# A hybrid encoder block on one core: the order of the first row blocks, the scale of V's second half, the queue of four stores, and the waits at the start of the MLP

## The chip, the cores and the metric

The kernel runs on one core of a Trainium2 chip. The metric is the device time of one execution in microseconds (us), given as the median of several runs. The engines are TensorE (PE in the profile; PEld are its weight loads), VectorE (DVE), ScalarE (ACT), GpSimd (POOL) and SyncE (SP, which here does nothing but issue DMAs). Each engine works through its own instruction queue strictly in program order; semaphores make it wait for the others. A wait at the head of a queue therefore holds everything behind it on that engine.

## The reference

One pre-norm encoder layer over 1024 tokens of width 1024, in float32. Cut to what matters:

```
u = rms_norm(x, norm1_g)
q, k, v, cb, cc, ch, ga, gb = split(u @ w_in)     # 512 columns each, ga and gb 1024
q, k = rms_norm(q) , rms_norm(k)                  # per head, 8 heads x 64
y_a = neighbourhood_attention(q, k, v, rpb) @ w_attn_branch
y_b = (cb * conv3(cc * ch)) @ w_conv_branch
x = x + (sigmoid(ga) * y_a + sigmoid(gb) * y_b) @ w_o
h = rms_norm(x, norm2_g) @ w_mlp_in               # 1024 x 1024 by 1024 x 4096
y = x + square(relu(h)) @ w_mlp_out               # 1024 x 4096 by 4096 x 1024
```

## The kernel before

**Numbers.** Every float32 operand of a matmul is split into two float16 parts, hi and lo, after a scaling by a power of two; a product is three passes (hi hi, hi lo, lo hi). ScalarE makes the hi part (a copy with scale, L291), VectorE the lo part (value times scale minus hi, L278). Tokens come in eight row blocks of 128; x is held in `xt`, its normed rows in `u16` (tile `u`), the turned rows, which the matmuls take, in `uT`.

**Weights.** A `Chunk` is a piece of a weight matrix, 2 to 4 raw tiles of up to 128x1024 float32. `Chunk.prep` (L230 to L293) makes the power of two for it and then its two parts. For V and the MLP the scale comes from the largest magnitude (VectorE scans each raw tile, L302); for the kinds Q, K, C and G it comes from the sum of squares (ScalarE squares each raw tile with an accumulated sum, L241; a tiny matmul with ones, `all_sum` L177 to L183, adds over the partitions; `gm2`, the square of the largest gain, bounds the result). V is two chunks (`half` 0 and 1). Of each of them GpSimd makes the lo part of the second raw tile, in two steps (scale, then subtract); VectorE makes that of the first. `Chunk.first`, `done` and `load_upto` let SyncE's queue issue the next weight loads as raw tiles come free: five raw buffers.

**The order.** It is written out by hand. Two lists of Python generators hold work for the vector engines: `bg` (weight chunks, advanced by `tick`) and `fg` (everything else, advanced by `step`). `unit` issues the matmuls of one group, then the late evictions of the unit before, and then so many steps and ticks. `apart(mark, n)` and `wait(n)` make a generator wait until n more units or steps have gone. So the numbers in the schedule decide where in each engine's queue an instruction stands.

**The beginning** (L515 to L562). `ln_step(b, n)` advances the norm of row block b: a square on ScalarE (L418), a chain of small VectorE operations (L391, L394, L396, L102, L400) with one ScalarE root (L392), the hi part of u on ScalarE (L421), the lo part on VectorE (L423). Blocks 0 to 2 are turned on TensorE (`ln_trans`, L429 to L435), blocks 3 to 7 by transposing DMAs (`ln_turn`). V's units (`v_unit`) are six of 256 columns, then five of 512; their results leave the PSUM banks by ScalarE (L509) and VectorE (L510). `sforms` (L468) makes, for four pairs of row blocks, the sums of rows that the gates' seven-product scheme needs: ScalarE scales the two xt blocks (L475), GpSimd adds (L481), ScalarE casts to hi (L483), VectorE makes lo (L485), and `sform_store` (L488) sends 1 MB to DRAM (`GS`). Then Q and K: eight units each of 24 matmuls, whose results ScalarE evicts (L578, L579, L596).

**The MLP's first half** (L1478 on). Weights and rows are combined so that one `quad` needs seven products instead of eight: `quad(q)` is seven groups of 12 matmuls, in the order 1, 6, 5, 4, 2, 7, 3, with its partial sums in the seven forms z[0] to z[6] of a tile `AS[q]` (two buffers, so quad q takes that of quad q-2). Quads 0 and 1 are done in two halves of 256 columns. After a quad's last group `h_done` (L1430) stands in `fg`: Relu and Square on ScalarE (L1432, L1434), then `sums` (L1159: four additions into forms 4 to 6, on VectorE for quads 0 and 1, on GpSimd later), then the store of all seven forms, 1792 KB, to `HS` from SyncE's queue (L1438). The buffer is free when the store has landed. Meanwhile the next weight chunks are prepared on ScalarE (L952, L961, L981), GpSimd (L966) and VectorE (L932, L933, L977), with `all_sum` (L179, L182) between.

Of the kernel before, what the change touches and what calls it, by code (L numbers as in the profile page):

```python
# [10 lines left out]
F32 = mybir.dt.float32  # L11
# [41 lines left out]
def encoder_block(ctx: ExitStack, tc: tile.TileContext, x, weights, cols, gqk, rel, masks, out):  # L53
# [166 lines left out]
    class Chunk:  # L220


        def __init__(self, kind, widths, tag, rows, half, more):
            self.kind, self.bank = kind, {"V": "o", "Q": "o", "K": "s", "C": "d"}.get(kind)
            self.tag, self.rows, self.widths, self.more = tag, rows, widths, more
            self.offs = []
            self.raw, self.ready, self.half, self.pool = [], more > 0, half, () if half is None else (1,)
            self.split = False

        def prep(self):  # L230
            n = len(self.widths)
            nk = sum(k for k, _ in self.widths)
            rm, a, b, s = (cols_of("prep", i) for i in (nk, 1, 1, 1))
            self.inv = keep()
            tot = sum(k * w for k, w in self.widths)
            if self.kind in "QKCG":
                self.parts = wsp.tile([128, 2, tot], F16, name="w16_ws", tag="ws")
                for p, (k, w) in enumerate(self.widths):
                    while len(self.raw) <= p:
                        yield WAIT  # L240
                    A.activation(self.parts[:, 1, :k * w].bitcast(BF16), self.raw[p][:, :k * w], AF.Square,  # L241
                                 accum_out=sc[:, at(rm, p)])
                    yield
                V.tensor_reduce(sc[:, a], sc[:, at(rm, 0, n)], axis=AX, op=OP.add)
                c = ones_col()
                V.tensor_tensor(c, sc[:, a], sc[:, gm2], op=OP.mult)
                yield from apart(units[0], 2 if self.kind == "Q" else 3)
                yield from all_sum(c, b, bank(self.bank) if self.bank else anybank(), 1e-36)
                yield from pow2_half(b, 14, s, self.inv, more=self.more)
            else:  # L250
                yield from self.largest(rm, a, b)
                yield from pow2(b, 14, s, self.inv, False, more=self.more)
            V.tensor_scalar(sc[:, rm], sc[:, self.rows], sc[:, s], None, op0=OP.mult)
# [15 lines left out]
            prev, scaled = None, {}  # L269
            for it in todo + [None]:  # L270
                if prev:
                    p, parts, f = prev
                    for o, m, c in parts:
                        hi, lo = (self.parts[:, w, f + o:f + o + m] for w in range(2))
                        if p in self.pool:
                            G.tensor_tensor(lo, scaled[p][:, o:o + m], hi, op=OP.subtract)
                        else:
                            V.scalar_tensor_tensor(lo, self.raw[p][:, o:o + m], sc[:, c:c + 1], hi,  # L278
                                                   op0=OP.mult, op1=OP.subtract)
                    done[0] += 1  # L280
                    load_upto(done[0] + 5)
                splitting[0] = True
                if it:
                    p, parts, f = it
                    if p in self.pool:
                        scaled[p] = w1p.tile([128, 1024], F32, name="scaled", bufs=1)
                        for o, m, c in parts:
                            G.tensor_scalar(scaled[p][:, o:o + m], self.raw[p][:, o:o + m], sc[:, c:c + 1], 1.0,
                                            op0=OP.mult, op1=OP.mult)
                    for o, m, c in parts:  # L290
                        A.activation(self.parts[:, 0, f + o:f + o + m], self.raw[p][:, o:o + m], AF.Copy,  # L291
                                     scale=sc[:, c:c + 1])
                prev = it  # L293
                self.split = it is None
                yield
# [191 lines left out]

    def sform_store(n, v):  # L488
        yield from apart(units[0], 1)
        SP.dma_start(GS[:, n], v)  # L490
        formed[0] = n + 1

    def ln_step(b, n=1):
# [19 lines left out]
                               for k in range(8) for sa, sw in PASSES]), post, steps, ticks)  # L513

    push(cV[0])  # L515
    ln_step(0, 2)
    tick()
    ln_step(0, 5)
    ln_step(1)
    tick(3)  # L520
    ln_step(0)
    ln_step(1)
    tick(4)
    ln_trans(u16[:, 0], 0, UT)
    flush()
    ln_step(1, 5)
    ln_step(1)
    ln_step(2, 2)
    push(cV[1])
    tick(1)  # L530
    v_unit(0, 0, 0, 0)
    ln_step(2, 4)
    ln_trans(u16[:, 1], 1, UT)
    ln_step(2, 1)
    tick(3)
    ln_step(2)
    tick(4)
    ln_step(3, 2)
    ln_trans(u16[:, 2], 2, UT)
    ln_step(3, 4)  # L540
    fg.append(qk_gain())
    fg.append(sforms())
    V.tensor_reduce(sc[:, gm2], sc[:, g1], axis=AX, op=OP.max, apply_absolute_value=True)
    mul(gm2, gm2, gm2)
    for p in range(11):
        if p == 3:
            flush()
            push(cQ)
        if 0 < p < 6:
            v_unit(p % 3, p // 3, 1, 2)  # L550
        elif p:
            v_unit(p - 3, None, 2, 4)
        for q in (p,) if p < 6 else (2 * p - 6, 2 * p - 5):
            c = q // 2 + 3
            if c < 8 and q % 2 == 0:
# [2 lines left out]
                turned[0] = c + 1  # L558
            if c < 7:
                ln_step(c + 1, 3)  # L560
    settle()
    flush()  # L562

# [624 lines left out]

    PART = ((0, 4), (4, 7))

    spare = []

    def pieces(n, part):

# [88 lines left out]
    def forms_m():  # L1283
# [9 lines left out]
        load_upto(done[0] + 5)  # L1293
        t2 = w4p.tile([128, 2, 512], F16, name="t2", bufs=1)
        t4 = w4p.tile([128, 2, 512], F16, name="t4", bufs=1)
        k4 = lambda v: v.rearrange("p (k c) -> p k c", k=4)
        flat = {0: lambda i: P1[0][:, 7, i], 1: lambda i: two[:, 0, i], 2: lambda i: two[:, 1, i],
                5: lambda i: t2[:, i], 6: lambda i: t4[:, i]}
# [130 lines left out]

    def h_done(q):  # L1430
        f = AS.pop(q)
        A.activation(f[:, 0:4], f[:, 0:4], AF.Relu)  # L1432
        yield
        A.activation(f[:, 0:4], f[:, 0:4], AF.Square, scale=sc[:, c1[q].inv],  # L1434
                     accum_out=sc[:, at(bsum[q // 4], q % 4)])
        yield
        yield from sums(f, G if q > 1 else V)
        SP.dma_start(HS[q // 4][:, :, q % 4], f)  # L1438
        live.remove(q)
# [7 lines left out]
    def quad(q, c0=0, c1=512):  # L1447
# [5 lines left out]
            AS[q] = w4p.tile([128, 7, 512], F32, name="as", tag="as")  # L1453
        ps = {}
        z = [AS[q][:, i, c0:c1] for i in range(7)]

        def post6(ps):
            V.tensor_tensor(z[5], ps[6], z[4], op=OP.add)  # L1458
# [280 lines left out]
```

## Time and profile before

| What | us |
|---|---|
| median of 3 runs | 1242.75 (1242.17 to 1243.26) |
| the profiled execution | 1241.45 |
| its span on the core | 1239.7 |
| TensorE busy | 1200.9 |
| VectorE busy | 930.0 |
| ScalarE busy | 765.2 |
| GpSimd busy | 425.5 |

The mean granted clock of TensorE over the span is 0.996 of full speed. The span is the time from the first to the last instruction in the trace; the execution's time is 1.75 us longer. In the rows of a timeline, the first number is the start, the second the duration of the group, then engine, line, operation, output<-inputs and shape; `x4` is the count; the bracket gives the idle time of that engine just before, and what ended it. In the rows of the windows come, for each engine, its busy time and its count of instructions, then the granted clock (1.00 is full), the share of the DMA engines and GB/s.

### The profile page before, as it was taken

The page shows a single profiled execution, that of the slowest core. Times are in us where ns is not written, and L with a number is a line of the kernel's source. Part 1 is how long each engine was busy: PE and PEld are TensorE (multiplying, and loading weights), DVE is VectorE, ACT ScalarE, POOL GpSimd, SP SyncE. Part 2 cuts the span into 40 slices and gives each one's busy share as a digit, 9 for nine tenths or more (in the row PEclk, how much of TensorE's full clock was granted, in tenths as well). Part 3 has the DMA queues.
Part 4 walks back from the last instruction along what each step waited for, and adds up shares of the span by engine and source line. Part 5 has one row for each costly group of instructions (what it writes and reads, how often), then busy time and mean ns, then how long its engine had stood idle before and what let it go on. Part 6 is the DMA issues. An engine that isn't in the chain of part 4 may idle for free.

```text
span 1239.7 us, 17066 instructions
## 1 busy us (share of the span) xinstructions
PE 1200.9 (97%) x6294; PEld 575.6 (46%) x6294; DVE 930.0 (75%) x1743; ACT 765.2 (62%) x1179; POOL 425.5 (34%) x289
## 2 busy tenths in 40 slices
PE   5989999999999999999999899999999999999998
PEld 3534444444444444444458344444444444444444
DVE  6668677988557777877877654564546999999997
ACT  6777577787474554536767877877765763645430
POOL 2440003111331111101003356556657473473562
PEclk8999999999999999999999999999999999999999
DMA  6557446656651211216096543553474744436202
GB/s 257 107 203 170 79 120 137 133 119 120 132 144 44 68 45 58 68 34 255 18 178 146 204 150 130 187 171 136 161 288 161 300 167 148 167 116 232 102 34 102
DMA packets 170868, 173.36 MB, mean 140 GB/s; under 512 B 131488, under 2 KB 132000, under 8 KB 166688
## 3 DMA queue, kind: packets, MB, share of 16 engines
q1 hardware_dynamic: 170784, 172.27, 47.0%
q8 instruction: 49, 0.80, 0.3%
q14 instruction: 35, 0.29, 0.1%
HBM read 102.51 MB, written 37.75 MB: 113 GB/s over the span
## 4 chain that ended last, share of the span: by engine, by line
PE 67%; DVE 18%; ACT 7%; issue 4%; DMA 1%; POOL 1%; SPq 0%; DVEq 0%; ACTq 0%; POOLq 0%
PE ps_d L188 26%; PE ps_s L188 20%; PE ps_o L188 18%; PE ps_d L859 3%; DVE sz L797 2%; DVE P L823 2%; DVE w_s L977 2%; DVE w_ws L278 1%; DVE ops L1572 1%; POOL sform L481 1%; DMA raw<-in_weights 1%; ACT w_ws L241 1%; ACT as L1432 1%; DVE sc L302 1%; DVE sg L1093 1%
## 5 line engine op out<-in xcount | busy, mean ns | idle before, releaser
L188 PEld LDWEIGHTS <-ops 128*128 128x128 f16 x1356 | 132.4, 98 | 159.5 <-issue 2.7
L188 PEld LDWEIGHTS <-w 128*128 128x128 f16 x1368 | 133.2, 98 | 145.7 <-issue 7.2
L859 PE MATMUL ps_d<-uT,w_ws 128*128 128x512 f16 x528 | 125.4, 379 | 0.0
L188 PE MATMUL ps_d<-ops 128*128 128x512 f16 (+1 forms) x528 | 118.4, 374 | 0.0
L188 PE MATMUL ps_s<-ops 128*128 128x512 f16 x492 | 113.2, 379 | 1.5 <-DVE ops L1572 1.1
L1563 ACT ACTIVATE ops<-hf,sc 128x2048 f16<-128x2048 f32 x26 | 52.0, 1998 | 93.7 <-PE ps_o L188 34.8
L966 POOL TENSOR_TENSOR tsum<-raw 128x512 f32<-128x512 f32 x28 | 45.5, 1637 | 156.5 <-ACT raw L952 145.8
L188 PEld LDWEIGHTS <-uT 128*128 128x128 f16 x648 | 65.0, 101 | 70.4 <-issue 5.6
L1159 POOL TENSOR_TENSOR as<-as 128x512 f32<-128x512 f32 x56 | 76.6, 1369 | 37.1 <-ACT as L1434 33.8
L188 PEld LDWEIGHTS <-w_s 128*128 128x128 f16 x588 | 56.8, 98 | 69.4 <-DVE w_s L977 1.9
L188 PE MATMUL ps_d<-u2x,w 128*128 128x512 f16 (+1 forms) x360 | 80.0, 372 | 0.0
L1565 DVE SCALAR_TENSOR_TENSOR ops<-hf,sc,ops 128x2048 f16<-128x2048 f32 x26 | 74.2, 2852 | 5.2 <-ACT ops L1563 5.2
L188 PE MATMUL ps_o<-ops 128*128 128x512 f16 x336 | 77.1, 379 | 0.0
L859 PEld LDWEIGHTS <-w_ws 128*128 128x128 f16 x528 | 50.8, 98 | 52.5
L188 PE MATMUL ps_o<-u2T,w 128*128 128x512 f16 (+1 forms) x324 | 71.7, 371 | 0.0
L952 ACT ACTIVATE raw<-raw,sc 128x256 f32<-128x256 f32 x172 | 70.8, 493 | 0.7 <-DMA raw<-in_weights 0.7
L966 POOL TENSOR_TENSOR gsum<-raw 128x512 f32<-128x512 f32 x14 | 18.9, 1371 | 131.7 <-issue 57.1
L981 ACT ACTIVATE w<-raw,sc 128x512 f16<-128x512 f32 (+1 forms) x28 | 24.6, 927 | 61.2 <-DVE sc L411 61.2
L188 PE MATMUL ps_s<-u2T,w 128*128 128x512 f16 (+1 forms) x252 | 54.2, 366 | 2.4 <-DVE as L1467 2.4
L1458 DVE TENSOR_TENSOR as<-ps_d,as 128x512 f32<-128x512 f32 (+1 forms) x15 | 10.1, 673 | 58.8 <-ACT as L1475 58.8
L806 ACT ACTIVATE sz<-sz,sc 128x384 f32<-128x384 f32 (+1 forms) x64 | 37.3, 582 | 26.9 <-DVE sc L797 13.5
L278 DVE SCALAR_TENSOR_TENSOR w_ws<-raw,sc,w_ws 128x512 f16<-128x512 f32 (+2 forms) x72 | 46.1, 690 | 2.4 <-ACT w_ws L291 2.4
(336 smaller groups left out, 2615.2 us busy)
## 6 DMA issues: line engine op xcount, KB each, us to landing
raw<-in_weights SPq DMA_DIRECT2D x89, 512.0 KB, 5.5
hs<-as SPq DMA_DIRECT2D x16, 1792.0 KB, 8.7
hf<-hs SPq DMA_DIRECT2D x26, 1024.0 KB, 6.5
w2x<-in_weights SPq DMA_DIRECT2D x16, 512.0 KB, 8.1
raw<-in_weights SPq DMA_DIRECT2D x16, 384.0 KB, 3.8
xt<-in_x SPq DMA_DIRECT2D x8, 512.0 KB, 9.9
gs<-s SPq DMA_DIRECT2D x4, 1024.0 KB, 6.2
x<-in_x SPq DMA_DIRECT2D x8, 512.0 KB, 10.0
```

The costliest lines, as they stand in the source:

```text
L188: T.matmul(ps, l, r, start=a, stop=b)
L278: V.scalar_tensor_tensor(lo, self.raw[p][:, o:o + m], sc[:, c:c + 1], hi, op0=OP.mult, op1=OP.subtract)
L797: V.tensor_tensor_reduce(z[:, :d["n"]], d["ps"][:, :d["n"]], bm, sc[:, cneg], 3.0e38, OP.add, OP.min, accum_out=sc[:, d["mx"]])
L806: A.activation(z, z, AF.Exp, scale=-1.0, bias=sc[:, d["mx"]], accum_out=sc[:, d["sm"]])
L823: V.scalar_tensor_tensor(d["lo"], d["z"][:, :d["n"]], sc[:, d["r"]], d["hi"], op0=OP.mult, op1=OP.subtract)
L859: T.matmul(ps, l, r, start=a, stop=b)
L952: A.activation(v, v, AF.Copy, scale=sc[:, at(g, 4 * i + k)])
L966: G.tensor_tensor(t[:, o], a, b, op=OP.add)
L977: V.scalar_tensor_tensor(o(1), w, sc[:, s], o(0), op0=OP.mult, op1=OP.subtract)
L1159: sub.tensor_tensor(z[o], z[a], z[b], op=op)
L1563: A.activation(P[:, 1, 0], hf, AF.Copy, scale=sc[:, Rs])
L1565: V.scalar_tensor_tensor(P[:, 1, 1], hf, sc[:, Rs], P[:, 1, 0], op0=OP.mult, op1=OP.subtract)
```

## The change

Five edits. (1) In the beginning the norm of row block 0 is run seven steps at once ahead of V's first chunk; block 1's scale chain and `gm2` come ahead of that chunk's splits; V's unit of block 1 is issued earlier, and the steps and ticks behind the later units are dealt out anew. (2) V's second chunk takes its scale from the sum of squares. (3) GpSimd's share of V's splits goes to VectorE. (4) The four stores to `GS` are issued by ScalarE instead of SyncE. (5) At the MLP's start, `h_done` waits some steps for quads 0 and 1, before the Relu and before the sums; quad 2 keeps its forms z[4] and z[5] in two tiles that are otherwise unused by then (`t2`, `t4`).

```diff
-            self.raw, self.ready, self.half, self.pool = [], more > 0, half, () if half is None else (1,)
+            self.raw, self.ready, self.half = [], more > 0, half
...
-            if self.kind in "QKCG":
-                self.parts = wsp.tile([128, 2, tot], F16, name="w16_ws", tag="ws")
+            if self.kind in "QKCG" or self.half:
+                self.parts = vhome[0][:, 1] if self.half else wsp.tile([128, 2, tot], F16, name="w16_ws", tag="ws")
...
-                yield from apart(units[0], 2 if self.kind == "Q" else 3)
-                yield from all_sum(c, b, bank(self.bank) if self.bank else anybank(), 1e-36)
+                if not self.half:
+                    yield from apart(units[0], 2 if self.kind == "Q" else 3)
+                yield from all_sum(c, b, bank(self.bank) if self.bank else anybank(), 1e-36, not self.half)
...
-                        if p in self.pool:
-                            G.tensor_tensor(lo, scaled[p][:, o:o + m], hi, op=OP.subtract)
-                        else:
-                            V.scalar_tensor_tensor(lo, self.raw[p][:, o:o + m], sc[:, c:c + 1], hi,
-                                                   op0=OP.mult, op1=OP.subtract)
+                        V.scalar_tensor_tensor(lo, self.raw[p][:, o:o + m], sc[:, c:c + 1], hi,
+                                               op0=OP.mult, op1=OP.subtract)
...
-        SP.dma_start(GS[:, n], v)
+        A.dma_start(GS[:, n], v)
...
     push(cV[0])
-    ln_step(0, 2)
+    ln_step(0, 7)
     tick()
-    ln_step(0, 5)
     ln_step(1)
     tick(3)
     ln_step(0)
     ln_step(1)
     tick(4)
     ln_trans(u16[:, 0], 0, UT)
+    ln_step(1, 4)
+    V.tensor_reduce(sc[:, gm2], sc[:, g1], axis=AX, op=OP.max, apply_absolute_value=True)
+    mul(gm2, gm2, gm2)
     flush()
-    ln_step(1, 5)
+    ln_step(1)
     ln_step(1)
     ln_step(2, 2)
     push(cV[1])
-    tick(1)
+    tick(2)
     v_unit(0, 0, 0, 0)
     ln_step(2, 4)
     ln_trans(u16[:, 1], 1, UT)
     ln_step(2, 1)
-    tick(3)
+    tick(1)
+    v_unit(1, 0, 0, 0)
+    tick(7)
     ln_step(2)
-    tick(4)
-    ln_step(3, 2)
+    ln_step(3, 1)
     ln_trans(u16[:, 2], 2, UT)
-    ln_step(3, 4)
+    tick(2)
+    ln_step(3, 5)
     fg.append(qk_gain())
     fg.append(sforms())
-    V.tensor_reduce(sc[:, gm2], sc[:, g1], axis=AX, op=OP.max, apply_absolute_value=True)
-    mul(gm2, gm2, gm2)
     for p in range(11):
...
-        if 0 < p < 6:
+        if p == 1:
+            step()
+            tick(2)
+        elif p and p < 6:
             v_unit(p % 3, p // 3, 1, 2)
-        elif p:
-            v_unit(p - 3, None, 2, 4)
+        elif p > 5:
+            v_unit(p - 3, None, 0, 4 if p < 7 else 8)
...
+        if p > 5:
+            step(2)
...
+        extra.extend(t.rearrange("p a c -> p (a c)").bitcast(F32) for t in (t2, t4))
...
     def h_done(q):
         f = AS.pop(q)
+        if q < 2:
+            yield from wait((3, 2)[q])
         A.activation(f[:, 0:4], f[:, 0:4], AF.Relu)
...
+        yield from wait((9, 3)[q] if q < 2 else 0)
         yield from sums(f, G if q > 1 else V)
         SP.dma_start(HS[q // 4][:, :, q % 4], f)
...
         z = [AS[q][:, i, c0:c1] for i in range(7)]
+        if q == 2:
+            z[4:6] = extra
```

More of the change, by code (lines that the diff above doesn't have):

```diff
@@ L268, in prep @@
                 o += k
-            prev, scaled = None, {}
+            prev = None
             for it in todo + [None]:
@@ L284, in prep @@
                     p, parts, f = it
[L285 to L289, printed above, removed]
                     for o, m, c in parts:
@@ L1189, in encoder_block @@
     PART = ((0, 4), (4, 7))
-    spare = []
+    spare, extra = [], []
     def pieces(n, part):
```

## The prediction

> **What bounds the kernel now.** I read the clock and span first, then the page's first part, then windows by stage, then the timelines of TensorE (PE), ScalarE (ACT), VectorE (DVE) and GpSimd (POOL) around each edit.
>
> ```profile
> span 1239.7 us, 17066 instructions
> ...
> PE 1200.9 (97%) x6294; PEld 575.6 (46%) x6294; DVE 930.0 (75%) x1743; ACT 765.2 (62%) x1179; POOL 425.5 (34%) x289
> ```
>
> PE is idle for 1239.7 - 1200.9 = 38.8 us. Only that idle time, and time at a low granted clock, can be won; what is lost must appear as new idle. The rows of the windows (from:to, length, then busy time of each engine, clock, DMA share, GB/s) show the two places that the change touches:
>
> ```profile
> 22.00:26.00 4.00, 2.03 (x18) 1.82 (x19) 3.53 (x11) 1.83 (x5) 0.15 (x1) 0.56 0.31 124
> ...
> 62.00:78.50 16.50, 11.34 (x50) 4.76 (x50) 11.87 (x14) 13.81 (x17) 7.97 (x6) 1.00 0.49 157
> 78.50:151.00 72.50, 72.50 (x339) 32.93 (x338) 53.92 (x150) 45.19 (x79) 6.86 (x6) 1.00 0.67 157
> ...
> 692.00:694.00 2.00, 2.00 (x7) 0.60 (x6) 0.00 (x0) 2.00 (x3) 1.27 (x1) 0.50 0.15 53
> ```
>
> From 62.0 to 78.5 PE idles 5.16 us; from 78.5 to 151 not at all. TensorE's timeline (start, length, operation, and in brackets the idle time before it) says what it waited for:
>
> ```profile
> 64.43 5.35 PE L188 MATMUL ps_s<-w_v,uT 128*128 128x512 f16 x24 [2.35 <-DMA uT<-u]
> 69.62 0.38 PE L188 MATMUL ps_d<-w_ws,uT 128*128 128x512 f16 x1
> 70.18 0.81 PE L188 MATMUL ps_d<-w_ws,uT 128*128 128x512 f16 x3 [0.19 <-DVE w_ws L278]
> 71.86 0.81 PE L188 MATMUL ps_d<-w_ws,uT 128*128 128x512 f16 x3 [0.88 <-DVE w_ws L278]
> 73.54 0.81 PE L188 MATMUL ps_d<-w_ws,uT 128*128 128x512 f16 x3 [0.87 <-DVE w_ws L278]
> 75.22 3.24 PE L188 MATMUL ps_d<-w_ws,uT 128*128 128x512 f16 x14 [0.87 <-DVE w_ws L278]
> ...
> 114.58 5.34 PE L188 MATMUL ps_d<-w_ws,uT 128*128 128x512 f16 x24
> ```
>
> V's last unit waits 2.35 us for the turned rows of block 7, and Q's first unit 0.19 + 0.88 + 0.87 + 0.87 = 2.81 us for Q's splits. So the begin can win at most about 5 us there. Q0 ends at 75.22 + 3.24 = 78.46, K0 (K's first unit) at 119.92.
>
> **The first 30 us.** Rows of ScalarE, then of VectorE:
>
> ```profile
> 18.12 1.04 ACT L418 ACTIVATE sq<-xt 128x1024 f32<-128x1024 f32 x1
> ...
> 30.86 3.29 ACT L291 ACTIVATE w_v<-raw,sc 128x256 f16<-128x256 f32 x8
> ```
>
> ```profile
> 12.78 2.46 DVE L278 SCALAR_TENSOR_TENSOR w_v<-raw,sc,w_v 128x256 f16<-128x256 f32 x4
> ...
> 31.47 1.67 DVE L278 SCALAR_TENSOR_TENSOR w_v<-raw,sc,w_v 128x256 f16<-128x256 f32 x4
> ```
>
> A low part by VectorE took 2.46/4 = 0.615 us beside POOL's splits and 1.67/4 = 0.417 us alone. Eight alone cost 3.34 us against 2.46 for four; but block 1's scale chain (some six operations) now stands ahead, so the splits start about 1.1 us later and V's first unit ends about 0.9 us later. I cost this at nothing: in 22 to 26 us PE is busy for 2.03 of 4.00 us, at a clock of 0.56, so it waits for block 1's rows there anyway; if that cover were gone, it would cost the 0.9. V's second scale moves two scans of 1024 columns from VectorE to two squares of about 1.2 us (18.12's row with its read) on ScalarE, +2.35 us there; since that scale no longer stands behind the blocks' chains, V's second splits start near 25.5, not 30.86.
>
> [...]
>
> **From V's last unit to K.** ScalarE's queue is the place that decides:
>
> ```profile
> 53.36 1.91 ACT L483 ACTIVATE s<-sform 128x2048 f16<-128x2048 f32 x1 [1.72 <-POOL sform L481]
> ...
> 57.26 1.13 ACT L421 ACTIVATE u<-xt,sc 128x1024 f16<-128x1024 f32 x1
> ...
> 63.94 1.91 ACT L483 ACTIVATE s<-sform 128x2048 f16<-128x2048 f32 x1 [4.58 <-POOL sform L481]
> 65.75 2.17 ACT L475 ACTIVATE xt<-xt,sc 128x1024 f32<-128x1024 f32 x2
> 68.34 2.56 ACT L291 ACTIVATE w_ws<-raw,sc 128x512 f16<-128x512 f32 x4 [0.42 <-DVE sc L253]
> ...
> 71.29 2.55 ACT L291 ACTIVATE w_ws<-raw,sc 128x512 f16<-128x512 f32 x4
> ...
> 74.65 1.91 ACT L483 ACTIVATE s<-sform 128x2048 f16<-128x2048 f32 x1 [0.34 <-POOL sform L481]
> ...
> 81.81 0.67 ACT L578 ACTIVATE qs<-ps_d,sc 128x512 f32<-128x512 f32 x1
> ...
> 85.98 1.91 ACT L483 ACTIVATE s<-sform 128x2048 f16<-128x2048 f32 x1 [1.03 <-POOL sform L481]
> ...
> 109.60 0.69 ACT L578 ACTIVATE qs<-ps_d,sc 128x512 f32<-128x512 f32 x1 [0.56 <-PE ps_d L188]
> ...
> 110.86 2.55 ACT L291 ACTIVATE w_ws<-raw,sc 128x512 f16<-128x512 f32 x4
> ```
>
> Before, the order is gate form 0 (53.36), scaling for form 1, block 7 (57.26), form 1 (63.94), scaling for form 2, Q's splits (68.34), form 2 (74.65), Q0's eviction (81.81). In the changed program block 7 stands ahead of form 0, and Q's splits ahead of form 1.
>
> The gain: block 7 near 55.5, so V's last unit starts near 63.1 (64.43 before), Q's splits near 63.5 and Q0 runs from 68.3 to 73.5 without a stall. PE leads by 78.46 - 73.5 = 4.9 us.
>
> The loss: eight splits and the two V evictions among them keep ScalarE until 69.05, so form 1 starts there, 5.1 us late. Then its 1.9 us, a store's issue, the scaling for form 2 (2.17) until 73.5, POOL's work on form 2 (5.2 us in the quiet case, 73.5 to 79.3 with its start), and form 2 on ScalarE at 79.3, 4.65 us after 74.65. Both programs evict Q0 behind form 2 and put K's splits behind Q6's eviction. Before, ScalarE stood late all the way: only at Q6 did it wait for PE (0.56), so from form 2 to K's splits it needed 110.86 - 74.65 - 0.56 = 35.65 us of its own chain. The 1.03 us wait at form 3 falls away. The moved stores come on top:
>
> ```profile
> L490 SPq DMA_DIRECT2D gs<-s x4: 332/384/989, 62.1 to 90.2; - x4
> ```
>
> ```profile
> 116.48 1.41 DVE L278 SCALAR_TENSOR_TENSOR w_ws<-raw,sc,w_ws 128x512 f16<-128x512 f32 x2
> ```
>
> An issue took SyncE's queue 332 to 989 ns (median 384). On ScalarE no row shows it; I bound it by 0 and 0.99 each and take 0.38, because the transfer is the same. Three lie between form 2 and K: 1.15 us. K's splits start at 79.3 + 35.65 - 1.03 + 1.15 = 115.1, 4.2 us later than before. PE, ahead by 4.9, has finished Q7 at 114.58 - 4.9 = 109.7 and waits until 115.1 + 1.28 (69.62 - 68.34, split to first matmul) = 116.4: 6.7 us idle that was not there. K's last low part ended at 117.89, 7.0 after the splits began: now 122.1, and with the last three matmuls (0.65) K0 ends at 122.7, +2.8. At Q0's pace (78.46 - 68.34 = 10.1 from split to end) it is 125.2, +5.3. Where PE had gaps like that, the clock stood at 0.56 for the 4 us of 22 to 26; four such microseconds do three of K0's eight pieces (three matmuls of 0.22 us each, twice as long at half clock: 1.3 us a piece), the other five take 3.25: 116.4 + 4 + 3.25 = 123.65. I take that, **begin +3.7 us** between 2.8 and 5.3, because a stretch with gaps is the nearest row. Whoever moves the splits or form 2 forward by some 3 us undoes it.
>
> Behind it nothing absorbs the shift: from 78.5 to 151 PE is 100% busy, so a shift of K0 is carried on whole. Moving the stores off SyncE's queue releases weight loads behind them, but no PE wait in 62 to 151 names a weight load.
>
> [...]
>
> **The MLP's start.** Rows of ScalarE, VectorE, SyncE's queue, the stores' landing, TensorE:
>
> ```profile
> 677.22 2.00 ACT L1434 ACTIVATE as<-as,sc 128x2048 f32<-128x2048 f32 x1
> ...
> 683.28 1.76 ACT L981 ACTIVATE w<-raw,sc 128x512 f16<-128x512 f32 x2 [3.70 <-DVE sc L411]
> ```
>
> ```profile
> 679.35 1.42 DVE L1159 TENSOR_TENSOR as<-as 128x512 f32<-128x512 f32 x2 [3.58 <-ACT as L1434]
> ...
> 682.34 0.15 DVE L182 TENSOR_SCALAR sc<-ps_d 128x1 f32<-128x1 f32 x1
> ```
>
> ```profile
> 682.50 0.62 SPq L1438 DMA_DIRECT2D hs<-as  x1
> ```
>
> ```profile
> DMA to landing us min/median/max: 6.5/8.7/9.0
> ```
>
> ```profile
> 690.39 4.23 PE L188 MATMUL ps_s<-u2T,w 128*128 128x512 f16 x12 [2.36 <-DVE as L1467]
> ...
> 699.42 0.16 PE L179 MATMUL ps_s<-ones 128*128 128x1 bf16 x1 [2.01 <-DVE ones L933]
> ...
> 717.60 2.75 PE L188 MATMUL ps_o<-u2T,w 128*128 128x512 f16 x12
> ```
>
> VectorE's sums for quad 0 (679.35, to 682.4) stand ahead of the scale of chunk 2 (682.34), whose splits make everything late: PE waits 2.36 us, does 12 matmuls in 4.23 instead of 2.75 us at a clock of 0.50, and waits 2.01 again: 5.85 us. With the new waits that scale is read at about 677.7, the splits on ScalarE begin after the squares at 679.55, 3.7 us earlier, and the 2.36, the slow clock and the 2.01 go. With quad 2's two forms in the spare tiles, no early form of it waits for store 0.
>
> But the sums come nine steps later, which by the units' steps falls behind quad 1's last post: about 686.9 to 689.7. Store 0 starts at 689.75 instead of 682.50. Its landing frees the buffer for quad 2's other forms, which VectorE writes in order. At 6.5 us (the smallest, of a store that went alone, as this one now does) it lands at 696.25; VectorE stands until then, with the next chunk's scale behind it, and PE waits at the next quads. By my step-by-step order, the group at 717.60 starts about 19 us after that landing, at 715.2: **-2.4 us**. At 8.5 us it is 717.2 (-0.4), at 5.0 us 713.7 (-3.9).
>
> [...] Here 2.36 us of idle stood ahead of a clock of 0.50, so the row decides, and the 1.5 us count as won. [...]
>
> **Sum.** 1241.45 (the profiled execution: 1239.7 of span and 1.75 around it) + 3.7 - 2.4 = 1242.75; the median of the three runs shown lies 1.3 above that execution, so 1244.05, rounded to 1244.1.
>
> **Rivals.** (1) *ScalarE's lag does not bind.* For it: ScalarE is busy 45.19 of 72.50 us there, and so a chain of evictions that starts late could catch up; against it: Q6 waited only 0.56 us. If K's splits begin by 109, the lead of 4.9 us stays: 1242.75 - 4.9 - 2.4 = 1235.5; with half of the lead 1237.9.
> (2) *Slower: K starves.* The place is ScalarE's queue between form 2 and K's splits. With K0 at Q0's pace (+5.3) and three issues of 0.99 instead of 0.38 (+1.8) K0 ends 7.1 later: 1242.75 + 7.1 - 2.4 = 1247.5; with a store 0 of 8.5 us, which leaves only 0.4 of the other gain, 1249.5. It decides from the moment that K's splits begin after 119.92 - 0.65 - 7.0 = 112.3, so form 2 after about 76.5.
> (3) *Nothing comes of it*: Q's splits stand ahead of form 1 in the program, but both lags stay as they were; VectorE's low parts and the squares lie beside PE's waits: 1242.75.
>
> **Chances.** A difference under 0.2% (2.5 us) can't be told from no change. Forecast (1241 to 1246.5) 0.45, of which 0.27 within 0.2% and 0.18 above; rival 1 0.28; rival 2 0.20; rival 3 0.07. So faster 0.28, same 0.34, slower 0.38. The range goes from rival 1's half lead, 1237.5, to 1249.0, short of rival 2's far end; it leaves out most of rival 1's whole lead and that end, some 0.2.
>
> **What would show it.** Right: Q0 without stall, ending near 73.5; form 2 on ScalarE near 79; K's splits near 115; 5 to 7 us of PE idle before K0 and a low clock after it; store 0 issued near 690 (before-time), the 2.36 gone, a new wait at quad 3. Wrong: K0 follows Q7 directly (rival 1), a landing of store 0 over 8 us, or a new wait of PE before 60 us.

## The result: 0.16% slower

The changed kernel takes 1244.8 us (median of 22 runs, 1243.32 to 1246.18) against 1242.74 us of the kernel before (22 runs, 1241.5 to 1244.26) in the same series: ratio 1.0016, 95% interval 1.0009 to 1.0022. That is a loss of 2.06 us, within the 0.2% that the prediction counts as "same", but clear of zero. The forecast was 1244.1 in a range of 1237.5 to 1249. The number held; the two terms behind it did not, as follows.

The profiled execution of the changed kernel took 1245.44 us:

```profile
span 1243.5 us, 17053 instructions
...
PE 1200.9 (97%) x6294; PEld 575.4 (46%) x6294; DVE 930.5 (75%) x1750; ACT 767.3 (62%) x1183; POOL 416.8 (34%) x273
```

TensorE is as busy as before (1200.9; matmuls at half clock count as busy too: 5.00 of 5.00 us at a clock of 0.50 in 719 to 724), so the 3.8 us by which this span is longer show as idle time. The windows of the changed kernel that answer to those shown of before, and those where the new idle time is:

```profile
62.00:78.50 16.50, 16.50 (x78) 7.46 (x77) 10.74 (x12) 11.17 (x15) 7.77 (x6) 1.00 0.61 225
100.00:130.00 30.00, 24.63 (x107) 10.60 (x106) 24.65 (x67) 22.11 (x39) 1.83 (x2) 0.89 0.75 163
112.00:116.00 4.00, 2.77 (x7) 0.92 (x7) 4.00 (x10) 3.92 (x9) 0.00 (x0) 0.50 0.11 25
...
719.00:724.00 5.00, 5.00 (x13) 1.78 (x12) 1.06 (x7) 3.82 (x5) 3.51 (x3) 0.50 0.02 9
```

The 5.16 us of idle in 62 to 78.5 are gone (16.50 of 16.50). In exchange 5.37 us are idle in 100 to 130, where before none was, and the clock is at 0.50 behind them. TensorE's timeline, begin and MLP:

```profile
61.05 5.34 PE L188 MATMUL ps_s<-w_v,uT 128*128 128x512 f16 x24
66.23 5.34 PE L188 MATMUL ps_d<-w_ws,uT 128*128 128x512 f16 x24
...
112.75 0.58 PE L188 MATMUL ps_d<-w_ws,uT 128*128 128x512 f16 x1 [4.89 <-ACT w_ws L284]
113.81 6.64 PE L188 MATMUL ps_d<-w_ws,uT 128*128 128x512 f16 x23 [0.48 <-DVE w_ws L276]
```

```profile
689.20 2.75 PE L188 MATMUL ps_s<-u2T,w 128*128 128x512 f16 x12
...
695.19 0.16 PE L179 MATMUL ps_s<-ones 128*128 128x1 bf16 x1 [0.65 <-DVE ones L933]
...
718.78 0.16 PE L179 MATMUL ps_s<-ones 128*128 128x1 bf16 x1 [5.28 <-DVE ones L933]
718.81 5.28 PE L188 MATMUL ps_o<-u2T,w 128*128 128x512 f16 x12
723.88 3.05 PE L188 MATMUL ps_d<-u2x,w 128*128 128x512 f16 x12
```

Q0 ends at 71.57 instead of 78.46: a lead of 6.9 us. At K0 it has been spent, and K0 ends at 120.45 against 119.92. In the MLP the first two waits go (2.36 to nothing, 2.01 to 0.65), but one of 5.28 us comes 24 us later, and the group behind it takes 5.28 instead of 2.75 us at a clock of 0.50. The next group starts at 723.88; before, the one behind the group at 717.60 started at 720.19. The distance has grown from 0.5 us at K0 to 3.7 us.

### The profile page after: what moved, and what is told of

Same layout as the page of the kernel before. It is cut to its first block, busy times and chain, and to the rows that moved or that the text cites. A ratio compares the mean times of both kernels' runs of the same rounds, so it can differ in the third digit from the quotient of the medians.

```text
span 1243.5 us, 17053 instructions
## 1 busy us (share of the span) xinstructions
PE 1200.9 (97%) x6294; PEld 575.4 (46%) x6294; DVE 930.5 (75%) x1750; ACT 767.3 (62%) x1183; POOL 416.8 (34%) x273
## 4 chain that ended last, share of the span: by engine, by line
PE 63%; DVE 21%; ACT 9%; issue 5%; DMA 1%; POOL 0%; DVEq 0%; ACTq 0%; SPq 0%; POOLq 0%
PE ps_d L188 24%; PE ps_s L188 19%; PE ps_o L188 16%; PE ps_d L859 3%; DVE sz L797 2%; DVE P L823 2%; DVE w_ws L276 2%; DVE w_s L977 2%; DVE ops L1578 1%; ACT w_ws L241 1%; DVE u L416 1%; ACT as L1435 1%; DVE sc L295 1%; DVE sg L1093 1%; DVE w L977 1%
## 5 line engine op out<-in xcount | busy, mean ns | idle before, releaser
L1571 DVE SCALAR_TENSOR_TENSOR ops<-hf,sc,ops 128x2048 f16<-128x2048 f32 x26 | 73.5, 2828 | 5.2 <-ACT ops L1569 5.2
L188 PE MATMUL ps_o<-u2T,w 128*128 128x512 f16 (+1 forms) x324 | 74.3, 380 | 0.0
L188 PE MATMUL ps_d<-w_ws,uT 128*128 128x512 f16 x192 | 44.6, 390 | 5.4 <-ACT w_ws L284 4.9
```

What stands on the lines that cost most here:

```text
L188: T.matmul(ps, l, r, start=a, stop=b)
L1571: V.scalar_tensor_tensor(P[:, 1, 1], hf, sc[:, Rs], P[:, 1, 0], op0=OP.mult, op1=OP.subtract)
```

## Experiments

**Theory A** by these rows: two separate losses. In the begin, K's splits come late on ScalarE and eat the lead; in the MLP, the late store of quad 0 holds VectorE, and TensorE starves behind it. **Theory B**: the MLP's waits gain what they seem to gain, and the begin loses it all. "Before" in the table is the kernel before in the same series of runs; a ratio below 1 is faster.

| run | median us | before | ratio, 95% interval |
|---|---|---|---|
| begin alone | 1244.50 | 1243.52 | 1.0010 (1.0001 to 1.0019) |
| MLP alone | 1243.84 | 1243.52 | 1.0003 (0.9994 to 1.0012) |
| store 0 in two parts | 1241.62 | 1243.52 | 0.9989 (0.9980 to 0.9998) |
| K's scale a unit earlier | 1244.04 | 1243.52 | 1.0005 (0.9997 to 1.0014) |
| form 2 behind Q1's eviction | 1248.17 | 1242.99 | 1.0041 (1.0028 to 1.0053) |
| sums' waits 3 and 6 | 1246.07 | 1242.99 | 1.0027 (1.0017 to 1.0036) |
| stores on SyncE again | 1245.86 | 1242.99 | 1.0020 (1.0010 to 1.0029) |
| form 2 behind Q1's eviction, with the waits 3 and 6 | 1249.78 | 1242.99 | 1.0052 (1.0040 to 1.0065) |
| two buffers for the forms | 1240.58 | 1243.06 | 0.9981 (0.9972 to 0.9990) |
| store 0 left out | 1240.36 | 1243.06 | 0.9986 (0.9977 to 0.9995) |
| parts 0, 1, 3 early and wait 6 | 1244.87 | 1243.06 | 1.0016 (1.0007 to 1.0025) |
| two buffers, store in two parts | 1235.94 | 1242.77 | 0.9953 (0.9939 to 0.9967) |

### The begin alone, the MLP alone

The first takes the MLP's edit out of the changed kernel, the second puts it alone into the kernel before:

```diff
     def h_done(q):
         f = AS.pop(q)
-        if q < 2:
-            yield from wait((3, 2)[q])
...
-        yield from wait((9, 3)[q] if q < 2 else 0)
...
-        if q == 2:
-            z[4:6] = extra
```

> The changed kernel with its MLP edit undone (the MLP starts as in the kernel before). Theory A (two losses: a lead of 6.7 us on Q is lost again at K's first unit by 5.4 us of waiting and 2.3 us of low clock; the MLP's waits lose about 3 us): K's first unit ends at 120.4 against 119.9 and the kernel is 0.3 to 0.8 us slower than before, ratio 1.0002 to 1.0007. Theory B (the waits at the start of the MLP are the gain they look like, and the loss is the begin's, by the moved stores and the DMAs that land later): 3 us slower or more, ratio above 1.002.

> The kernel before with the MLP edit alone. Theory A: TensorE's waits at the start of the MLP grow from 4.4 to about 6 us, with one group at half clock, and the time rises by 2 to 3.5 us, ratio 1.0016 to 1.0028. Theory B: the edit gains about 2 us, ratio 0.998. If the 0.9 us wait for the turned rows at 665 us shows here too, it belongs to neither part.

Measured: 1.0010 and 1.0003. Neither is the gain that theory B needs, and neither is the whole loss; both intervals are wide against what was to be told apart. Theory A's price of 2 to 3.5 us for the MLP alone is outside its interval too (-0.7 to 1.5 us). The traces say more. With the begin alone K0 ends at 121.16, 1.2 us late. Its MLP, which is that of the kernel before, looks like this on TensorE:

```profile
692.31 4.23 PE L188 MATMUL ps_s<-u2T,w 128*128 128x512 f16 x12 [2.45 <-DVE as L1467]
...
701.34 0.16 PE L179 MATMUL ps_s<-ones 128*128 128x1 bf16 x1 [2.21 <-DVE ones L933]
701.37 4.44 PE L188 MATMUL ps_o<-u2T,w 128*128 128x512 f16 x12
```

Both waits of before are there, and here the group behind the second one runs at half clock too (4.44 us); in the profiled execution of before it took 2.75. So the old schedule's own price at this place was 5.9 us in one execution and about 7.8 here. The MLP alone:

```profile
717.57 0.16 PE L179 MATMUL ps_s<-ones 128*128 128x1 bf16 x1 [5.32 <-DVE ones L933]
717.59 5.10 PE L188 MATMUL ps_o<-u2T,w 128*128 128x512 f16 x12
```

The wait of 5.3 us and the slow group are there without any change of the begin: they belong to the MLP's edit alone. What they cost depends on what they are held against. From the start of quad 2 to the group behind the slow one it takes 39.9 us in the changed kernel and 39.5 here; with the begin alone, under the old schedule, it takes 39.3, and in the profiled execution of before 37.5. Against the profiled execution of before this span is 2.1 us longer (1241.8 against 1239.7), by the medians 0.3 us; the difference is largely that execution's own luck, which lay 1.3 below its median. The wait for turned rows at 665 us shows in both (0.65 and 0.32 us) and lies between 0 and 0.91 in the other runs: it belongs to neither part.

### The moved stores

```diff
-        A.dma_start(GS[:, n], v)
+        SP.dma_start(GS[:, n], v)
```

> The changed kernel with the four stores of the gates' forms issued from SyncE's queue again. Theory A (an issue from ScalarE's queue lies beside its running instructions and costs nothing there, and the stores hold nobody): same time as the changed kernel within 0.5 us, K's splits start at 112.0 within 0.3 us. The price of 0.38 us for each, as put in the prediction's sum, would make them start 1.1 us earlier. Rival (stores in SyncE's queue hold weight loads behind them, since they wait for VectorE): a new wait of TensorE for weights and 1 us or more lost.

Half of theory A was wrong here (the stores do hold somebody), and so was the prediction's term. SyncE's queue, then GpSimd and ScalarE, in the run with the stores on SyncE; the changed kernel's ScalarE for comparison:

```profile
66.09 4.90 SPq L210 DMA_DIRECT2D raw<-in_weights  x4
71.04 23.94 SPq L483 DMA_DIRECT2D gs<-s  x4
```

```profile
76.90 1.27 POOL L474 TENSOR_TENSOR sform<-xt,sform 128x512 f32<-128x512 f32 x1
```

```profile
79.86 1.91 ACT L476 ACTIVATE s<-sform 128x2048 f16<-128x2048 f32 x1 [6.99 <-DMA gs<-s]
```

```profile
61.85 2.56 ACT L284 ACTIVATE w_ws<-raw,sc 128x512 f16<-128x512 f32 x4 [2.47 <-DVE sc L254]
...
64.86 0.38 ACTq L483 DMA_DIRECT2D gs<-s  x1
...
67.24 1.90 ACT L476 ACTIVATE s<-sform 128x2048 f16<-128x2048 f32 x1
...
77.51 1.91 ACT L476 ACTIVATE s<-sform 128x2048 f16<-128x2048 f32 x1 [5.33 <-POOL sform L474]
...
84.67 0.67 ACT L578 ACTIVATE qs<-ps_d,sc 128x512 f32<-128x512 f32 x1
...
111.99 2.54 ACT L284 ACTIVATE w_ws<-raw,sc 128x512 f16<-128x512 f32 x4
```

On SyncE store 0 stands behind four weight loads, which go out only as Q's splits free raw buffers (66.09 to 71.0): it leaves at 71.04. On ScalarE it leaves at 64.86, while the splits run (the issue lies inside their time). Form 2's cast takes over store 0's buffer, so on SyncE it also waits for that landing and comes at 79.86 instead of 77.51. Not all of the 6.99 us is the store's: GpSimd ended form 2 only at 78.17, so the landing adds 1.7 us; and this execution was 0.7 us late already at Q's splits (62.54 instead of 61.85), before any of these stores. From form 2 to K's splits it then took 34.97 us instead of 34.48, and the 0.49 us between them is a longer wait for a DMA of Q's rows (0.87 instead of 0.38 at that step). So the chain is as long with the issues in ScalarE's queue as without them: they cost nothing there. K0 ends at 116.65 + 6.98 = 123.63, 3.2 us later than in the changed kernel, of which about 2 belong to the stores' place. The medians of the two (ratios 1.0020 and 1.0016) do not tell them apart; the spans differ by 1.3 us. What the move gains at K0 is an earlier landing of store 0: on SyncE it leaves 6.18 us later, behind the four loads, and the cast that waits for its landing starts 8.82 us after its issue (79.86 - 71.04); issued by ScalarE it landed 4.9 us after its issue.

### What eats the lead: four trials

K's scale one unit earlier:

```diff
-                    yield from apart(units[0], 2 if self.kind == "Q" else 3)
+                    yield from apart(units[0], 2 if self.kind in "QK" else 3)
```

> The changed kernel, with K's scale read one unit of matmuls earlier, so that K's splits stand behind Q5's eviction instead of Q6's. Theory A (K's splits, behind the late evictions, are what eats the lead): splits start at about 107.7 instead of 112.0, K's first unit ends near 117 instead of 120.45, and the time falls by 3 to 4 us against the changed kernel, about 1241. Rival (the evictions that now stand behind the splits hold the banks, and TensorE waits at K's third or fourth unit instead): no gain.

The splits start at 108.70 (111.99 in the changed kernel), but Q6's eviction now stands between them, and TensorE waits four times, 4.05 us together, the last time here:

```profile
118.44 1.26 PE L188 MATMUL ps_d<-w_ws,uT 128*128 128x512 f16 x5 [1.66 <-DVE w_ws L276]
```

K0 ends at 119.70, 0.75 us earlier instead of 3 to 4. Not decisive: the late evictions are in the way wherever the splits stand. So the evictions themselves had to come earlier. Form 2's cast behind Q1's eviction:

```diff
-            yield from apart(start, 2)
+            yield from apart(start, 5 if n == 2 else 2)
...
-            for b in (n, n + 4):
+            for b in {2: (2, 6, 3, 7), 3: ()}.get(n, (n, n + 4)):
```

> The changed kernel, with form 2 cast three units of matmuls later on ScalarE (behind Q1's eviction instead of ahead of Q0's) and the scalings for form 3 done together with those for form 2. Theory A (the lead on Q is lost because Q's evictions stand in ScalarE's queue behind form 2, which waits for GpSimd until 77.5): Q0 is evicted near 72 instead of 84.7, K's splits start near 104 instead of 112.0, K's first unit follows Q7 with under 1 us of waiting and at full clock, ending near 114 instead of 120.45, and the time falls by 5 to 7 us against the changed kernel. Rival (the chain of small steps between an eviction and the next sets the pace, whatever stands ahead of it): K's first unit ends above 118, gain under 2.5 us.

Missed: 1.0041 instead of a gain. Q0 is evicted at 77.57 instead of 84.67; but form 3 has become the late one, and TensorE waits longer than ever:

```profile
93.36 1.91 ACT L477 ACTIVATE s<-sform 128x2048 f16<-128x2048 f32 x1 [6.34 <-POOL sform L475]
```

```profile
115.92 0.58 PE L188 MATMUL ps_d<-w_ws,uT 128*128 128x512 f16 x1 [8.25 <-ACT w_ws L284]
```

A fourth form has to be out before Q's fourth unit is left (the schedule waits for it), and GpSimd can start form 3 only when form 2 has left the one buffer. To move the cast back moves form 3 back with it. The other way is to make form 2 early, with two changes at once: a second buffer, and each form's scalings one form earlier. Then GpSimd need wait neither for the buffer of form 1 nor for the scaled rows, which both come behind Q's splits:

```diff
-            for b in (n, n + 4):
+            for b in ((0, 4), (1, 5, 2, 6), (3, 7), ())[n]:
                 A.activation(xt[:, b], xt[:, b], AF.Copy, scale=sc[:, at(ys, b)])
+            for b in (n, n + 4):
                 z += [xt[:, b, :512], xt[:, b, 512:]]
-            f = wqk.tile([128, 4, 512], F32, name="sform", bufs=1)
+            f = (w1p if n % 2 else wqk).tile([128, 4, 512], F32, name="sform", bufs=1)
```

> The changed kernel, with two buffers instead of one for the sums of the gates' forms and the scalings of each form one form earlier, so that GpSimd can add up form 2 right behind form 1. Theory A (the lead on Q is lost because form 2's cast, ahead of Q0's eviction on ScalarE, waits for GpSimd until 77.5): the cast of form 2 comes at about 72.5, Q0's eviction near 78 instead of 84.7, K's splits near 104 to 106 instead of 112.0, K's first unit waits under 2 us and ends at 113 to 115 instead of 120.45; 5 to 7 us less than the changed kernel. Rival (GpSimd's place does not matter, the order of evictions and the rows' DMAs do): form 2 comes early, but K's splits stay above 110, gain under 2 us.

GpSimd, ScalarE and TensorE of this run:

```profile
69.10 1.60 POOL L475 TENSOR_TENSOR sform<-xt,sform 128x512 f32<-128x512 f32 x1
```

```profile
71.70 2.18 ACT L468 ACTIVATE xt<-xt,sc 128x1024 f32<-128x1024 f32 x2
...
74.74 1.90 ACT L477 ACTIVATE s<-sform 128x2048 f16<-128x2048 f32 x1
...
107.83 2.54 ACT L284 ACTIVATE w_ws<-raw,sc 128x512 f16<-128x512 f32 x4
```

```profile
110.67 5.34 PE L188 MATMUL ps_d<-w_ws,uT 128*128 128x512 f16 x24
```

GpSimd starts form 2 at 64.40 instead of 72.29 and is done with it at 70.70 instead of 77.48, and the cast no longer waits. By the rows of the changed kernel it needs both changes: there the scaled rows are ready at 71.2, and VectorE, which makes form 1's lo part, leaves the buffer at 72.15. Neither was tried alone. K's splits start 4.2 us earlier than in the changed kernel, K0 follows Q7 without a wait at full clock and ends at 116.01, 4.4 us earlier than in the changed kernel (113 to 115 was expected; Q's splits start at 64.51 instead of 61.85, and Q0's stalls of 0.64 + 0.87 + 0.87 us are back). The time is 1240.58; ratio to the kernel before 0.9981, where the changed kernel has 1.0016: 4.3 us less (5 to 7 was expected). That shows where most of the lead went: into the wait for form 2 ahead of all evictions, whose order is the same here. Of the 4.2 us at K's splits 2.8 are form 2's earlier cast; the other 1.4 lie between form 2 and the splits (33.09 us instead of 34.48), where form 3's scaling (2.18 us, here at 71.70) no longer stands.

### What holds the MLP: four trials

The changed kernel's VectorE, the store's issue and its landing:

```profile
678.99 0.16 DVE L182 TENSOR_SCALAR sc<-ps_d 128x1 f32<-128x1 f32 x1 [0.85 <-PE ps_d L179]
...
688.24 5.71 DVE L1159 TENSOR_TENSOR as<-as 128x512 f32<-128x512 f32 x4
...
700.69 0.69 DVE L1469 TENSOR_TENSOR as<-ps_s,t 128x512 f32<-128x512 f32 x1 [5.55 <-DMA hs<-as]
```

```profile
693.98 11.91 SPq L1442 DMA_DIRECT2D hs<-as  x2
```

```profile
688.05 1.28 POOL L966 TENSOR_TENSOR tsum<-raw 128x512 f32<-128x512 f32 x1 [0.32 <-ACT raw L952]
690.34 3.06 POOL L966 TENSOR_TENSOR tsum<-tsum,raw 128x512 f32<-128x512 f32 x2 [1.01 <-ACT tsum L961]
```

The four sums take 5.71 us; before, four took 1.42 + 1.41. Three of them run beside GpSimd's additions and take 1.64 each; the one that starts in GpSimd's pause (689.33 to 690.34) takes 0.69. Minimum, median and maximum in ns:

```profile
L1159 DVE TENSOR_TENSOR as<-as x4: 691/1636/1640, 688.2 to 692.3; 128x512 f32<-128x512 f32 x4
```

So the store leaves at 693.98, and VectorE stands until 700.69 with everything behind it. To test that the store is the cause, it was left out (quad 5's forms are written a second time in its place, so the second half of the MLP gets wrong values):

```diff
-        SP.dma_start(HS[q // 4][:, :, q % 4], f)
+        if q:
+            SP.dma_start(HS[q // 4][:, :, q % 4], f)
+        if q == 5:
+            SP.dma_start(HS[0][:, :, 0], f)
```

> The changed kernel without the store of quad 0's forms; quad 5 is stored a second time in its place, so the second half of the MLP reads wrong values in the same amount. Theory A (the landing of store 0 is what VectorE stands for): the 5.6 us wait is gone, the scale of chunk 4 is read at about 699.8 instead of 702.6, then held by quad 1's sums, TensorE's wait ahead of quad 3's second group falls from 5.3 to 2 to 3 us, the group behind it runs at full clock, and 3 to 5 us are gained. Rival (it is quad 1's sums and Squares ahead of that scale): the scale moves by less than 1 us and the time stays.

```profile
716.35 0.16 PE L179 MATMUL ps_s<-ones 128*128 128x1 bf16 x1 [2.38 <-DVE ones L933]
716.37 2.75 PE L188 MATMUL ps_o<-u2T,w 128*128 128x512 f16 x12
```

As theory A said: 5.28 becomes 2.38, the group behind runs in 2.75, and the ratio is 0.9986 where the changed kernel has 1.0016: 3.7 us less (the two profiled executions lie 5.2 apart). In the traces the store accounts for 2.9 us of waiting and, through the clock, for 2.5 more; the other 2.4 us are held by quad 1's Squares and sums ahead of the next chunk's scale (VectorE waits 2.66 us for ScalarE there). The same store in two parts:

```diff
+        a = 0
+        if q == 0:
+            a = 2
+            SP.dma_start(HS[0][:, 0:2, 0], f[:, 0:2])
         yield from wait((9, 3)[q] if q < 2 else 0)
         yield from sums(f, G if q > 1 else V)
-        SP.dma_start(HS[q // 4][:, :, q % 4], f)
+        SP.dma_start(HS[q // 4][:, a:, q % 4], f[:, a:])
```

> The changed kernel, with the store of quad 0 in two: forms 0 and 1 right behind the Square, the other five behind the sums. Theory A (VectorE stands 5.6 us because quad 2's second form waits for the landing of the late store): that wait goes, the scale of the next chunk is read about 3 us earlier, TensorE's wait of 5.3 us shrinks to about 2.4, and the time falls by 3 to 5 us against the changed kernel, about 1240.5. Rival (the sums of quad 1 and the Squares ahead of that scale hold it anyway): VectorE waits for ScalarE instead, less than 1 us gained.

```profile
699.07 0.69 DVE L1473 TENSOR_TENSOR as<-ps_s,t 128x512 f32<-128x512 f32 x1 [3.80 <-DMA hs<-as]
```

```profile
717.17 0.16 PE L179 MATMUL ps_s<-ones 128*128 128x1 bf16 x1 [3.53 <-DVE ones L933]
717.19 2.75 PE L188 MATMUL ps_o<-u2T,w 128*128 128x512 f16 x12
```

The time came out as expected (ratio 0.9989 where the changed kernel has 1.0016: 3.4 us less), but not quite for the reason given. VectorE still waits, 3.80 us: quad 2's second form lies in the part that left early (issued at 681.22, landed 3.1 us later), yet it waits for the whole buffer. What helped is that the second part is smaller and lands 4.8 us after its issue instead of 6.6. TensorE's wait fell by only 1.75 us; the rest is the clock, which was not throttled behind 3.53 us in this execution. It need not be so in each: the eleven executions have mean clocks of 0.992 to 0.997 and take 1240.5 to 1244.8 us.

The other way is to let the sums go earlier, while GpSimd is idle:

```diff
-        yield from wait((9, 3)[q] if q < 2 else 0)
+        yield from wait((3, 6)[q] if q < 2 else 0)
```

> The changed kernel, with the waits ahead of the sums 3 steps instead of 9 for quad 0 and 6 instead of 3 for quad 1: three of quad 0's four sums stand ahead of the splits of chunk 3, while GpSimd is idle, and quad 1's stand behind the scale of the next chunk. Theory A (the loss is the late store 0 and what VectorE holds behind it): the sums take 0.7 us each instead of 1.64, the store leaves near 688.5 instead of 694, VectorE does not wait for it by more than 1 us, TensorE's wait of 5.3 us and the half clock behind it go, at the price of about 1 us ahead of quad 2's third group: 4 to 6 us less than the changed kernel, near 1239.5. Rival (the first waits of the edit are the loss, the sums' place does not matter): no gain.

```profile
692.13 0.61 SPq L1442 DMA_DIRECT2D hs<-as  x1
692.84 13.98 SPq L210 DMA_DIRECT2D raw<-in_weights  x3
712.47 10.56 SPq L1442 DMA_DIRECT2D hs<-as  x2
```

```profile
701.06 0.69 DVE L1469 TENSOR_TENSOR as<-ps_s,t 128x512 f32<-128x512 f32 x1 [6.65 <-DMA hs<-as]
```

```profile
719.56 0.60 ACT L1481 ACTIVATE as<-ps_o 128x512 f32<-128x512 f32 x1 [2.44 <-DMA hs<-as]
```

Slower, 1.0027. Two sums got ahead of the splits, not three; the other two fell beside GpSimd again (2.65 us), ahead of an eviction by VectorE for which TensorE then waits 1.93 us at quad 2. Quad 2 starts at 685.68 here and at 684.02 in the changed kernel; counted from there, store 0 left 3.5 us earlier but landed only 1.3 us earlier, since it took 8.8 us with weight loads issued beside it. And quad 1's store left at 712.47 instead of 705.4, so that ScalarE's first copy for quad 3, which takes that buffer, waits 2.44 us. TensorE's wait there is 4.74 us, with half clock behind it. In the last trial the store went in parts 0, 1, 3 and 2, 4 to 6, and quad 1's sums waited 6 steps:

```diff
+        if q == 0:
+            SP.dma_start(HS[0][:, 0:2, 0], f[:, 0:2])
+            SP.dma_start(HS[0][:, 3, 0], f[:, 3])
-        yield from wait((9, 3)[q] if q < 2 else 0)
+        yield from wait((9, 6)[q] if q < 2 else 0)
```

> The changed kernel with quad 0's store in two parts, forms 0, 1 and 3 behind the Square and forms 2, 4, 5, 6 behind the sums, and 6 instead of 3 steps of wait ahead of quad 1's sums, so that the next chunk's scale stands ahead of them. Theory A (both the landing and quad 1's sums hold that scale): it is read at about 699.5, the splits begin at 700.5 instead of 704.1, TensorE's wait shrinks from 5.3 to about 2 us at full clock behind it, 4 to 6 us less than the changed kernel and about 1 us less than with forms 0 and 1 alone in the first part. Rival (the smaller second store lands no earlier, since weight loads run beside it, as in the run with 3 and 6 steps): no better than that run with two parts.

```profile
710.89 10.56 SPq L1449 DMA_DIRECT2D hs<-as  x2
```

```profile
718.08 0.60 ACT L1488 ACTIVATE as<-ps_o 128x512 f32<-128x512 f32 x1 [2.54 <-DMA hs<-as]
```

The scale is read at 700.09 and the splits begin at 701.02, each 0.5 us behind what was expected; but quad 1's store now leaves at 710.89 (705.4 in the changed kernel), and quad 3 waits for that one, as in the trial before: TensorE's wait is 5.05 us again, and the time 1244.87. A later store moves the wait one quad on. A third buffer for quads 0 to 2 might end it; it was not tried.

### Together

Form 2 behind Q1's eviction and the waits 3 and 6, each of which lost, were also run together:

> The edits of the run before the last two and of the last but one together: form 2 behind Q1's eviction, and the sums' waits 3 and 6. Theory A: the two places are independent, both gains add, about 10 us less than the changed kernel, near 1235, and 7 to 8 us less than the kernel before. Rival (what is gained at the begin is given back at a later wait, as at 172 to 300 us, where TensorE waits 7.5 us in both kernels): the gain at the begin is gone before 300 us, and only that of the MLP stays, near 1239.5.

They lose together as they do apart: 1.0052. The two that gained, on the changed kernel:

> The two edits that gained by themselves, together: two buffers for the gates' forms (1240.6 against 1243.1 of the kernel before) and quad 0's store in two parts (1241.6 against 1243.5), on the changed kernel. Theory A (two separate places): K's first unit has no wait, and TensorE's wait ahead of quad 3's second group is about 3.5 us at full clock instead of 5.3 and half clock; both gains add, 4 to 5 us beyond the two-buffer run's own loss at the MLP, about 1237, ratio 0.994 to 0.997 to the kernel before. Rival (the earlier arrival shifts the MLP's weight loads and stores against each other): no faster than 1240.

```profile
712.00 0.16 PE L179 MATMUL ps_s<-ones 128*128 128x1 bf16 x1 [3.54 <-DVE ones L934]
712.02 2.75 PE L188 MATMUL ps_o<-u2T,w 128*128 128x512 f16 x12
```

K0 follows Q7 at once (at 110.49), and behind a wait of 3.54 us the clock stays full. 1235.94 us, ratio 0.9953 (0.9939 to 0.9967): 6.8 us faster than the kernel before, where the changed kernel is 2.06 slower. What the change moved was worth moving in both places; the begin needed a second buffer and earlier scalings with it, the MLP a smaller store.

## Why the prediction was right, point by point

The time was right by luck: two errors of opposite sign met. Against the profiled execution of before, the begin's term was 3.2 us too high and the MLP's 4.8 too low; 0.8 us more wait for turned rows came in between, and 0.3 later. So this execution lies 4.0 above that one (1245.44 against 1241.45) where 1.3 was forecast. By the medians it is 2.06, since that execution lay 1.3 below its median and this one lies 0.6 above.

- **The first 30 us: half right.** VectorE's eight low parts came as worked out (3.25 us for eight alone). "At nothing" was not quite it: TensorE is idle 16.38 us in the first 60, 1.2 more than before (15.19), and waits there for low parts rose from 0.33 to 1.25 us: so the prediction's third sign of being wrong, a new wait before 60 us, did show. But in 18.5 to 30 the clock was 0.92 on the mean instead of 0.70, which outweighs it, and V's last unit started at 61.05, 2 us earlier than forecast.
- **The lead: right in kind, too small.** Q0 without a stall, ended at 71.57 (forecast 73.5): a lead of 6.9 us, not 4.9.
- **The lag: right in mechanism, too large.** Form 1 at 67.24 (69.05), form 2 at 77.51 (79.3), K's splits at 111.99 (115.1). From form 2 to the splits it took 34.48 us: 35.65 - 1.03 = 34.62 without any price for the issues. The price of 0.38 us for an issue on ScalarE fell: it costs nothing there, and the stores on SyncE would have cost about 2 us at K0.
- **K0: right in kind.** 4.89 + 0.48 us of idle and a clock of 0.50 behind it, as the text drew it; the first matmul came 0.76 us after the first split, not 1.28. K0 ended 0.53 us late in this execution instead of 3.7; in the profiled executions of the five other runs with the same begin it ended 1.2 to 2.1 us late. The rival "ScalarE's lag does not bind" was wrong: it did bind, and with most of it gone (the run with two buffers) K0 ended 3.9 us earlier than in the kernel before.
- **The MLP: the step that failed.** Up to the start of the sums everything came as written. This execution is 1.33 us late there; less that, the scale is read at 677.66 (forecast 677.7), the splits begin at 679.6 (679.55), the sums at 686.9 (686.9). The 2.36 us, the half clock and most of the 2.01 went. The failing step is "about 686.9 to 689.7. Store 0 starts at 689.75": it took the sums' 0.7 us from rows where GpSimd was idle. Beside GpSimd three of the four took 1.64 each, the store left 2.9 us later than that (again less the 1.33), and its landing (6.6 us, forecast 6.5) shifted with it. From the landing to quad 3's second group it took 18.2 us (forecast about 19), so that this group started 0.1 us earlier than before, not 2.4. The second omission is the clock: behind the new wait it was halved, and that group took 2.5 us more. So the term is +2.4 against the profiled execution of before, not -2.4.
- **The basis.** That execution had only one throttled group in the MLP where another of the same schedule had two, 1.7 us apart; against that other one the MLP of the changed kernel takes 0.6 us more, and by the medians its edit costs 0.3 us (-0.7 to 1.5). So it is shown that the forecast gain of 2.4 did not come; that the edit loses is not shown by the medians.

## What to carry to other kernels

A step that is shifted on one engine meets other neighbours: take its duration from rows where the engine that it will run beside is busy, not from where it ran before (0.69 us for a sum in GpSimd's pause, 1.64 beside its additions). A lead won on the bound engine was not kept here by moving one queue that feeds it (6.9 us at Q0, nothing at K0); look for the first buffer with a single copy between them, and for work on the way that could stand elsewhere. Store 0, issued 2.9 us later than forecast, landed about as much later (VectorE stood 5.55 us for its buffer): before moving a store, find who takes its buffer next, and whether a part of it can go first.

## What the runs showed of the hardware that was not expected

- Whether TensorE's clock falls behind a gap does not follow from the gap's length alone. In the MLP, behind 2.36, 2.45 and 2.21 us it was halved (12 matmuls in 4.23 to 4.44 us), behind 2.01 us in before, 2.38 us with store 0 left out and 3.53 and 3.54 us with the store in two parts it was not (2.75 us); behind 4.7 to 5.3 us the group was slow each time (4.35 to 5.28 us in nine runs). So gaps of 2.2 us were throttled here and gaps of 3.5 us were not.
- A 128x512 float32 addition of quad 0's sums on VectorE took 0.69 us in GpSimd's pause and 1.64 us beside GpSimd's additions, a factor of 2.4; for the low parts of 128x256 in the begin of the kernel before the two figures are 0.417 us alone and 0.615 us beside GpSimd's splits, a factor of 1.5.
- The 1792 KB store landed 6.6 us after its issue when no load was issued beside it, and 8.8 us after it with three weight loads issued behind it.
